# Letting the halves of a weight stream take turns at several byte places of their buffers

## The chip, the core and the metric

The kernel runs on one core of a Trainium2 chip. The metric is the device time of one execution in microseconds (us). The kernel before takes 1099.93 us, the median of 3 runs (1099.71 to 1100.56). The engines are named as in the profile: PE is the matrix engine (TensorE), PEld its weight load, DVE the vector engine, ACT the scalar engine, POOL the general-purpose engine (GpSimd), SP the engine whose queue issues most transfers.

## The reference: what is computed

Two layers of a decoder trunk over 256 tokens of width 1024, all in f32. Each layer does

```
x = x + W_out( sum_i sigmoid(G_i(h)) * P_i(mixer_i(h)) )     h = rmsnorm(x), four mixers, one wide projection w_in
x = x + cross_attention(rmsnorm(x), rmsnorm(mem))            4 heads, 256 memory tokens
x = x + (relu(rmsnorm(x) @ w_up)**2) @ w_down                hidden width 4096
```

and a last rmsnorm ends the trunk. Nearly all of the arithmetic is products of a 1024-wide (or 4096-wide) weight with the 256 tokens. The mixers (latent attention, a gated MLP over chunks, gated linear attention, a delta-rule network) add many small products and elementwise steps.

## The kernel before, in words

**The weight stream.** All large weights lie in one array in the order in which they are used, 168 halves of 128 x 1024 f32 in each layer, two halves to a transfer of 1 MB. The function `half()` hands out the next one. It takes a buffer `wh` and a buffer `wl` (four of each in rotation). ACT copies the raw half into `wh` in the format fp32r that PE multiplies (L191), DVE writes what is left over, raw minus `wh`, into `wl` (L194). A product in nearly full f32 precision is then three matmuls, `mm3` at L197 to L200: `wh` with the operand's high part, `wh` with its low part, `wl` with its high part. PE loads the 128 x 128 weights anew for each matmul.

**The products.** `gemm` takes the weights as the stationary side and streams 256 tokens of the operand past them: 8 chunks of 128 columns in a half, three matmuls each, so 24 matmuls of 128x256 to a half. `gemm_tok` turns the sides round: 128 tokens are stationary and 512 columns of the weights stream past, 12 matmuls of 128x512 to a half. The operands (`hh`, `hl`, `ah`, `al`, `mh`, `ml`, `brh`, `oh` and so on) are tiles of 2048 bytes in each partition.

**The places.** A `wh` or `wl` buffer has 1024 floats and 512 bytes of slack in each partition, 4608 bytes. The half lies in it at an offset of 0 to 480 bytes, the place. `PLACE` has one place for each stage and layer, `weights(stage)` sets it when the stage begins, and `half()` uses it for `wh` and `wl` alike. The buffers are nine times 512 bytes apart, a chunk of weights is 512 bytes long, the two halves of an operand tile are 1024 bytes and the tiles of one pool 2048 bytes apart. So within a stage the distance in bytes from the weights of a matmul to the operand that streams past them is the same for all, up to multiples of 512, and the place alone sets it.

**The stages**, with their halves in each layer and their places before, in bytes (layer 0, layer 1). All but tok, v and the second layer's down are `gemm`:

| stage | halves | what | place before | matmuls |
|---|---|---|---|---|
| z | 18 | input projections of the mixers | 384, 256 | 432 of 128x256 |
| tok | 6 | token-major projections, two small factors of the attention | 448, 448 | 48 of 128x512, some of 128x256 |
| gate | 32 | branch gates, interleaved with the mixers' small work | 256, 384 | 768 of 128x256 |
| k | 8 | keys of the memory | 128, 384 | 192 of 128x256 |
| br | 8 | branch projections | 384, 256 | 192 of 128x256 |
| out, q, o | 8 each | output, queries, attention output | 288, 352, 416 and 224, 480, 288 | 192 of 128x256 each |
| v | 8 | values of the memory | 448, 0 | 96 of 128x512 |
| up | 32 | MLP, first matrix | 384, 256 | 768 of 128x256 |
| down | 32 | MLP, second matrix | 256, 448 | layer 0: 768 of 128x256; layer 1: 384 of 128x512 |

**What sets the order.** A scheduler orders the instructions of each engine at build time. The splits of L191 and L194 have raised priority, so that they run ahead of their use. Transfers of the stream are issued from SP's queue. The mixers run as generators beside the gate stage: only there are the large products interleaved with many small ones.

Of the kernel before, what the change touches and what calls it, by code (L numbers as in the profile page):

```python
# [42 lines left out]
PAD = 48  # L43


SLACK = 512
PLACE = [
    dict(z=384, tok=448, gate=256, k=128, br=384, out=288, q=352, v=448, o=416, up=384, down=256),
    dict(z=256, tok=448, gate=384, k=384, br=256, out=224, q=480, v=0, o=288, up=256, down=448),
]  # L50
N_PIECE = 44

# [12 lines left out]
def decoder(ctx: ExitStack, tc: tile.TileContext, ws, xn_d, xt_d, mem_d, pos_d, fin_d, par_d, cst_d, msk_d, out_d):  # L65
# [12 lines left out]
    def nm(s):  # L78
        uid[0] += 1
        return f"{s}_{uid[0]}"  # L80
# [59 lines left out]
    for j in range(4):  # L140
        c = slice(1024 * (j % 2), 1024 * (j % 2) + 1024)
# [27 lines left out]
    class Stream:  # L169
        i = 0  # L170
        raw = None
        place = PLACE[0]["z"]

    def half(parts=1):
        if Stream.i % 2 == 0:
            if Stream.i < 4:
                Stream.raw = raw0[Stream.i // 2]
            else:
                Stream.raw = wp.tile([P, 2048], F32, tag="wr", name=nm("wr"), bufs=3)
                nc.sync.dma_start(Stream.raw, ws[Stream.i // 2])  # L180
        o = 1024 * (Stream.i % 2)
        Stream.i += 1
        r = Stream.raw[:, o : o + 1024]
        wh, wl = (wp.tile([P, 1024 + SLACK // 4], F32R, tag=n, name=nm(n), bufs=4) for n in ("wh", "wl"))
        b = Stream.place // 4
        wh, wl = wh[:, b : b + 1024], wl[:, b : b + 1024]
        n = 1024 // parts
        for c in range(0, 1024, n):
            p = slice(c, c + n)
            with tc.high_priority(offset=WP):  # L190
                i = S.activation(wh[:, p], r[:, p], AF.Copy)  # L191
                if Stream.i <= 4:
                    tc.keep_in_program_order(i)
                V.tensor_tensor(wl[:, p], r[:, p], wh[:, p].bitcast(F32), op=ALU.subtract)  # L194
        return wh, wl
# [6 lines left out]
    def lead4(xh, xl, evac, pieces):  # L202

        bk = [pg.tile([P, 2, T], F32, tag="g", name=nm("g")) for _ in range(2)] + [bank() for _ in range(2)]
        for j in range(4):
            w = half(2 if j == 0 else 1)
            pieces(j)
            for m in range(4):
                for i in range(2):
                    k = 2 * j + i  # L210
                    c = slice(256 * m + 128 * i, 256 * m + 128 * i + 128)
                    mm3(bk[m][:, 0], w[0][:, c], w[1][:, c], xh(k), xl(k), k == 0, k == 7)
        for p in range(2):
            evac(p, [(slice(m, m + 1), bk[2 * p + m][:, 0:1]) for m in range(2)])

    def gemm(xh, xl, nk, npair, evac, lead=False, tail=False, first=0):

        for p in range(first, npair):  # L220
            apart = (lead and p == 0) or (tail and p == npair - 1)
            if apart:
                bk = [pg.tile([P, 2, T], F32, tag="g", name=nm("g")) for _ in range(2)]
                parts = [(slice(m, m + 1), bk[m][:, 0:1]) for m in range(2)]
                out = [bk[m][:, 0] for m in range(2)]
            else:
                ps = pg.tile([P, 2, T], F32, tag="g", name=nm("g"))
                parts = [(slice(0, 2), ps)]
                out = [ps[:, m] for m in range(2)]
            if lead and p == 0:  # L230
                w = [half() for _ in range(2)]
                order = [(m, k) for kp in range(0, 8, 2) for m in range(2) for k in (kp, kp + 1)]
            else:
                w = [None, None]
                order = [(m, k) for m in range(2) for k in range(nk)]
            for m, k in order:
                if k % 8 == 0 and not (lead and p == 0):
                    w[m] = half()
                c = slice(128 * (k % 8), 128 * (k % 8) + 128)
                mm3(out[m], w[m][0][:, c], w[m][1][:, c], xh(k), xl(k), k == 0, k == nk - 1)  # L240
            evac(p, parts)
# [196 lines left out]
    def layer(l):  # L438
# [18 lines left out]
        def weights(stage):  # L457
            Stream.place = PLACE[l][stage]

# [1010 lines left out]
```

## Time and profile before

| what | value |
|---|---|
| median of 3 runs | 1099.93 us |
| the profiled execution's own time | 1101.14 us |
| its span from first to last instruction | 1098.5 us |
| granted clock of PE over the span | 0.996 |
| busy: PE, PEld, DVE, ACT, POOL | 98%, 94%, 74%, 53%, 18% |
| read from HBM | 182.75 MB, 167 GB/s over the span |

The profile is one execution. A row of the view of groups names line, engine, operation, output<-inputs and shape, then the count, the busy time in us with the mean of one in ns, and the idle time of the engine just before. Matmuls are pipelined: each has a duration of some 280 ns, and yet the next one starts after some 115 ns, so the rate is read from how many start in a stretch of time, not from durations. The view of stretches gives for each stretch (us from the span's start) its length, PE's busy time and the number of its instructions that overlap the stretch, the granted clock, the share of the DMA engines and what they moved.

### The profile page before, as it was taken

How to read it: one execution, taken by the hardware profiler on the slowest of the kernel's cores; microseconds unless marked ns; L12 is line 12 of the kernel's file. 1: busy time of each engine (PE TensorE's matmuls, PEld its weight loads, DVE VectorE, ACT ScalarE, POOL GpSimd, SP SyncE). 2: the span in 40 equal slices, each digit the busy share in tenths (PEclk: the TensorE clock that was granted, in tenths of full speed). 3: DMA queues.
4: the chain of work that ended last, by engine and by line, in shares of the span. 5: the costliest groups of instructions: out<-in, count | busy, mean ns of one | idle time of the engine just before them, and what ended most of it. 6: DMA issues, size and time to landing. Idle time of an engine off the chain costs nothing.

```text
span 1098.5 us, 20696 instructions
## 1 busy us (share of the span) xinstructions
PE 1074.4 (98%) x8494; PEld 1032.4 (94%) x8494; DVE 812.5 (74%) x1419; ACT 584.2 (53%) x875; POOL 194.6 (18%) x170
## 2 busy tenths in 40 slices
PE   8989999999999999999999999999999999999996
PEld 8979998899998999999999899999999899999885
DVE  6999857779866876655679997686797768665454
ACT  6565554554645655544454746554455555555342
POOL 6234005108200200000101420320351001010000
PEclk9999999999999999999999999999999999999999
DMA  9442523354544455555545444244445345554551
GB/s 354 163 179 111 204 104 121 110 193 156 191 153 154 154 192 192 192 192 193 192 183 192 155 154 154 103 150 151 174 177 204 122 152 193 186 194 177 192 192 38
DMA packets 28319, 185.13 MB, mean 169 GB/s; under 512 B 3392, under 2 KB 3648, under 8 KB 6976
## 3 DMA queue, kind: packets, MB, share of 16 engines
q1 hardware_dynamic: 26208, 179.09, 44.9%
q10 hardware_dynamic: 2016, 4.72, 1.3%
q8 instruction: 66, 1.08, 0.4%
q14 instruction: 29, 0.24, 0.1%
HBM read 182.75 MB, written 1.05 MB: 167 GB/s over the span
## 4 chain that ended last, share of the span: by engine, by line
PE 86%; DVE 8%; ACT 2%; DMA 2%; issue 1%; POOL 0%; DVEq 0%; ACTq 0%
PE g L198 25%; PE g L199 25%; PE g L200 25%; DVE wl L194 2%; DMA mr<-memt 1%; PE ps L198 1%; PE ps L199 1%; PE ps L200 1%; ACT wh L191 1%; PE ps L666 1%; PE ps L662 1%; DVE cv L539 1%; DVE qt L861 0%; DMA wr<-ws 0%; PE ps L972 0%
## 5 line engine op out<-in xcount | busy, mean ns | idle before, releaser
L194 DVE TENSOR_TENSOR wl<-wr,wh 128x1024 fp32r<-128x1024 f32 (+1 forms) x337 | 416.9, 1239 | 187.8 <-ACT wh L191 186.6
L191 ACT ACTIVATE wh<-wr 128x1024 fp32r<-128x1024 f32 (+1 forms) x337 | 355.1, 1057 | 344.3 <-PE g L199 238.8
L200 PE MATMUL g<-hh,wl 128*128 128x256 f32 x1152 | 325.1, 282 | 3.5 <-DVE wl L194 3.5
L198 PE MATMUL g<-hh,wh 128*128 128x256 f32 x1152 | 323.8, 282 | 1.9 <-ACT gt L1097 1.4
L199 PE MATMUL g<-hl,wh 128*128 128x256 f32 x1152 | 322.9, 280 | 0.0
L200 PEld LDWEIGHTS g<-hh,wl 128*128 128x128 f32 x1152 | 216.5, 188 | 5.5 <-DVE wl L194 4.5
L198 PEld LDWEIGHTS g<-hh,wh 128*128 128x128 f32 x1152 | 216.5, 188 | 3.1 <-ACT gt L1097 1.8
L199 PEld LDWEIGHTS g<-hl,wh 128*128 128x128 f32 x1152 | 217.3, 189 | 0.4 <-issue 0.2
L338 POOL TENSOR_TENSOR sq<-sq,sq 128x512 f32<-128x512 f32 x14 | 21.2, 1513 | 350.5 <-ACT sq L330 350.3
L198 PE MATMUL g<-xh,wh 128*128 128x256 f32 x272 | 75.5, 281 | 2.0 <-ACT xh L311 2.0
L199 PE MATMUL g<-xl,wh 128*128 128x256 f32 x272 | 75.8, 281 | 0.0
L200 PE MATMUL g<-xh,wl 128*128 128x256 f32 x272 | 74.9, 280 | 0.0
L198 PE MATMUL g<-ah,wh 128*128 128x256 f32 x256 | 70.7, 276 | 0.0
L199 PE MATMUL g<-al,wh 128*128 128x256 f32 x256 | 70.7, 276 | 0.0
L200 PE MATMUL g<-ah,wl 128*128 128x256 f32 x256 | 70.7, 276 | 0.0
L198 PEld LDWEIGHTS g<-xh,wh 128*128 128x128 f32 x272 | 51.3, 190 | 2.4 <-ACT xh L311 2.4
L1113 POOL TENSOR_TENSOR gt<-gt,gt 128x512 f32<-128x512 f32 x16 | 35.6, 2228 | 91.0 <-DVE gt L1112 90.0
L199 PEld LDWEIGHTS g<-xl,wh 128*128 128x128 f32 x272 | 51.2, 189 | 0.1
L200 PEld LDWEIGHTS g<-xh,wl 128*128 128x128 f32 x272 | 51.0, 189 | 0.0
L200 PE MATMUL g<-wh,al 128*128 128x512 f32 x128 | 49.5, 389 | 0.0
L199 PE MATMUL g<-wl,ah 128*128 128x512 f32 x128 | 49.5, 389 | 0.0
L198 PE MATMUL g<-wh,ah 128*128 128x512 f32 x128 | 49.4, 390 | 0.0
(500 smaller groups left out, 2332.6 us busy)
## 6 DMA issues: line engine op xcount, KB each, us to landing
wr<-ws SPq DMA_DIRECT2D x166, 1024.0 KB, 4.8
wr<-ws ACTq DMA_DIRECT2D x4, 512.0 KB, 7.6
mr<-memt ACTq DMA_DIRECT2D x8, 256.0 KB, 4.5
par<-par SPq DMA_DIRECT2D x2, 778.0 KB, 7.0
x<-xt SPq DMA_DIRECT2D x3, 256.0 KB, 7.7
cst<-cst SPq DMA_DIRECT2D x1, 588.0 KB, 8.7
gf<-fin SPq DMA_DIRECT2D x2, 256.0 KB, 5.3
yt<-yg ACTq DMA_DIRECT2D x2, 256.0 KB, 2.5
```

What stands on the lines that cost most here:

```text
L191: i = S.activation(wh[:, p], r[:, p], AF.Copy)
L194: V.tensor_tensor(wl[:, p], r[:, p], wh[:, p].bitcast(F32), op=ALU.subtract)
L198: PE.matmul(out, ah, bh, start=start, stop=False)
L199: PE.matmul(out, ah, bl, start=False, stop=False)
L200: PE.matmul(out, al, bh, start=False, stop=stop)
L338: G.tensor_tensor(acc, acc, sq, op=ALU.add)
L539: V.scalar_tensor_tensor(cv[:, c, d], zc[p][:, c, 0 : T - 3 + k], col(o + k), cv[:, c, d], op0=ALU.mult, op1=ALU.add)
L662: PE.matmul(xp[:, h], M[:, h], Tm[:, h], start=True, stop=True)
L666: PE.matmul(up[:, h], X[t][:, h], U[:, h], start=True, stop=True)
L1113: G.tensor_tensor(gt[m][0], gt[m][0], gt[m][1], op=ALU.add)
```

## The change

The place becomes a list of pairs for each stage. Each half takes the next entry of its stage's list, by its number in the stream: the first number of a pair is the place of `wh`, the second that of `wl`. A list of one entry is a fixed place; a list of two or four makes the halves take turns. The sizes of the buffers stay as they are.

```diff
 SLACK = 512
+ONE, TOK = [(256, 256)], [(448, 448)]
 PLACE = [
-    dict(z=384, tok=448, gate=256, k=128, br=384, out=288, q=352, v=448, o=416, up=384, down=256),
-    dict(z=256, tok=448, gate=384, k=384, br=256, out=224, q=480, v=0, o=288, up=256, down=448),
+    dict(z=[(0, 0), (256, 256)], tok=TOK, gate=[(256, 256), (384, 384)], k=[(0, 0), (128, 128)], br=[(128, 128), (384, 384)],
+         out=ONE, q=ONE, v=TOK, o=ONE, up=[(256, 384)], down=[(0, 0), (128, 128), (256, 256), (384, 384)]),
+    dict(z=[(256, 256), (384, 384)], tok=TOK, gate=[(0, 256)], k=[(384, 384), (0, 0)], br=[(0, 0), (256, 256)],
+         out=ONE, q=ONE, v=TOK, o=ONE, up=[(0, 0), (256, 256)], down=TOK),
 ]
...
-        b = Stream.place // 4
-        wh, wl = wh[:, b : b + 1024], wl[:, b : b + 1024]
+        b, c = (n // 4 for n in Stream.place[Stream.i % len(Stream.place)])
+        wh, wl = wh[:, b : b + 1024], wl[:, c : c + 1024]
```

In the built program every engine has the same instructions in the same order as before, with the same shapes. Only the addresses differ from which matmuls read their weights (or, in `gemm_tok`, their streamed side) and to which L191 and L194 write.

By stage: two places 256 bytes apart take turns in z of layer 0, in br of both layers and in up of layer 1. Two places 128 bytes apart (384 and 0 are 128 apart, up to a multiple of 512) take turns in gate and k of layer 0 and in z and k of layer 1; down of layer 0 goes round four places in steps of 128. In gate of layer 1 and up of layer 0 the place is fixed, and `wh` and `wl` lie at different ones, 256 and 128 bytes apart. The stages out, q and o are at a fixed 256 in both layers, tok, v and the second layer's down at 448; of these v of layer 1 (0 before) is moved, tok and down are not.

## The prediction

> **What bounds the kernel now.** I read the page's busy times first, then its chain of waits by line, then the groups, and last the stretches, which decided.
>
> ```profile
> PE 1074.4 (98%) x8494; PEld 1032.4 (94%) x8494; DVE 812.5 (74%) x1419; ACT 584.2 (53%) x875; POOL 194.6 (18%) x170
> PE g L198 25%; PE g L199 25%; PE g L200 25%; DVE wl L194 2%; DMA mr<-memt 1%; PE ps L198 1%; PE ps L199 1%; PE ps L200 1%; ACT wh L191 1%; PE ps L666 1%; PE ps L662 1%; DVE cv L539 1%; DVE qt L861 0%; DMA wr<-ws 0%; PE ps L972 0%
> L200 PE MATMUL g<-hh,wl 128*128 128x256 f32 x1152 | 325.1, 282 | 3.5 <-DVE wl L194 3.5
> L198 PE MATMUL g<-hh,wh 128*128 128x256 f32 x1152 | 323.8, 282 | 1.9 <-ACT gt L1097 1.4
> L200 PE MATMUL g<-ah,wl 128*128 128x256 f32 x256 | 70.7, 276 | 0.0
> ```
>
> Three quarters of the span are the three matmuls of `mm3` one behind the other, with next to no idle time before them. So the time is the number of these matmuls times their spacing, and the change can only act on the spacing. The last two rows hint that it isn't one number: the matmuls on `ah` have a mean of 276 ns, those on `hh` 282, in the same shape.
>
> The stretches give it exactly. Each row is a piece of a stage with little in it but the large matmuls: its length, PE busy (so many instructions), clock, DMA share, GB/s. A matmul lasts some 280 ns, so about two that began earlier are counted at the left edge; I take the length over the count less two.
>
> ```profile
> 20.00:35.00 15.00, 15.00 (x130) 1.00 0.82 308
> 42.00:56.00 14.00, 14.00 (x126) 1.00 0.51 185
> 223.00:243.00 20.00, 20.00 (x173) 1.00 0.62 213
> 255.00:265.00 10.00, 10.00 (x87) 1.00 0.59 209
> 278.00:291.00 13.00, 13.00 (x112) 1.00 0.49 173
> 298.00:315.00 17.00, 17.00 (x144) 1.00 0.53 186
> 363.00:373.00 10.00, 10.00 (x88) 1.00 0.68 224
> 380.00:460.00 80.00, 80.00 (x681) 1.00 0.52 188
> 466.00:551.00 85.00, 85.00 (x753) 1.00 0.53 188
> 567.00:582.00 15.00, 15.00 (x135) 1.00 0.39 141
> 584.00:601.00 17.00, 17.00 (x148) 1.00 0.62 219
> 649.00:656.00 7.00, 7.00 (x64) 1.00 0.16 46
> 663.00:672.00 9.00, 9.00 (x80) 1.00 0.47 171
> 755.00:780.00 25.00, 25.00 (x215) 1.00 0.49 176
> 813.00:826.00 13.00, 13.00 (x112) 1.00 0.47 167
> 832.00:850.00 18.00, 18.00 (x154) 1.00 0.53 194
> 896.00:908.00 12.00, 12.00 (x104) 1.00 0.53 180
> 916.00:1000.00 84.00, 84.00 (x715) 1.00 0.53 192
> ```
>
> The two long ones: up of layer 0 (380 to 460) runs at 80/679 = 117.8 ns, down of layer 0 (466 to 551) at 85/751 = 113.2 ns. Clock, DMA share and GB/s are alike, so neither throttle nor transfers part them. At places that are multiples of 128 (all but out, q, o) every row is near one of these two values: z of layer 0 first 117.2 then 112.9, z of layer 1 112.8 then 116.4, gate of layer 1 112.9 then 115.4, k 117.0 and 117.4, br of layer 0 117.6, up of layer 1 117.8. I call them the **fast** and the **slow rhythm**, 4.6 ns apart. At the odd places out, q and o have rates of their own: layer 0 118.2, 119.7, 116.3; layer 1 118.2, 118.4, 117.6 ns.
>
> Two things matter for a change of places. First, one fixed place carries both rhythms (z and gate of layer 1), so the place doesn't fix the rhythm; where the stream was thrown decides. Second, a change of place throws it, even without a pause. At 465.5 us up hands over to down, place 384 to 256, and no idle time stands in the groups of the stretch 455 to 475:
>
> ```profile
> L200 PE MATMUL g<-hh,wl 128*128 128x256 f32 x31 | 8.6, 279 | 0.0
> L198 PE MATMUL g<-hh,wh 128*128 128x256 f32 x30 | 8.4, 280 | 0.0
> L198 PE MATMUL g<-ah,wh 128*128 128x256 f32 x28 | 7.7, 276 | 0.0
> ```
>
> The mean falls from 279 or 280 (slow) to 276 (fast) with the first matmuls of down, and stays there for the whole stage. A pause throws it too. In up of layer 1 the stream is fast until small matmuls of a statistic come between, and slow behind them:
>
> ```profile
> 909.79 0.28 PE L200 MATMUL g<-oh,wl 128*128 128x256 f32 x1
> 909.91 0.28 PE L198 MATMUL g<-hh,wh 128*128 128x256 f32 x1
> 910.02 0.28 PE L199 MATMUL g<-hl,wh 128*128 128x256 f32 x1
> 910.13 0.28 PE L200 MATMUL g<-hh,wl 128*128 128x256 f32 x1
> ...
> 914.33 0.50 PE L352 MATMUL ps<-cst,sq 128*128 128x1 f32 x4
> ...
> 915.48 0.28 PE L198 MATMUL g<-hh,wh 128*128 128x256 f32 x1
> 915.60 0.28 PE L199 MATMUL g<-hl,wh 128*128 128x256 f32 x1
> 915.72 0.28 PE L200 MATMUL g<-hh,wl 128*128 128x256 f32 x1
> ```
>
> These are starts in us. From the handover on (o at 288 to up at 256, between 909.79 and 909.91) the steps are 0.11, after the statistic at 914.33 they are 0.12. No change of place follows in that stage, and it stays slow to its end (916 to 1000).
>
> **The change part by part.** No instruction comes, goes or moves on any engine or queue, and no wait is added. The new addresses of L191 and L194 lie under PE's work: in the row of busy times DVE has 26% and ACT 47% of the span free, and all waits on L194 in the largest group are 3.5 us. I cost them at nothing; if every split became slower by 10 ns and none of it were hidden, 336 splits would be 3.4 us. What is left is the spacing, stage by stage. A half has 24 matmuls, so moving one stage of 768 from slow to fast is worth 768 x 4.6 ns = 3.5 us, one of 192 is worth 0.9.
>
> *Turns that differ by 128 bytes* throw the stream once in each half, every 2.8 us. Down of layer 0 shows that the fast rhythm, once reached, holds for 768 matmuls at a fixed place. The open question is whether it also survives a throw. Nothing before shows a throw out of the fast rhythm by a 128-byte step; the one throw by 128 from slow with a clear end went to fast (465.5 us), while gate to k in layer 0 (256 to 128) ends in the slow k of row 223 to 243. If throws from slow sometimes reach fast, and fast survives them, the turns work as a ratchet. Bounds: k of both layers are slow throughout (rows 223 and 755), 2 x 0.9 = 1.8 us; z of layer 1 and gate of layer 0 are partly fast, I take half slow, (432 + 768)/2 x 4.6 = 2.8 us; up of layer 0, where `wl` lies 128 from `wh` so that each triple is thrown, 3.5 us. All of it is 8.1 us, none of it is 0, and a loss is not excluded: the fast half of z and gate (2.8 us) and all of down (3.5 us) could fall to slow. I take three quarters of the gain, 6.1 us, and no loss in down, because the only clear throw ended fast and the turns give many tries.
>
> *Turns that differ by 256 bytes* (z and gate of one layer each, br twice, up of layer 1). From k to br in layer 0 the place goes 128 to 384, and the slow rhythm goes on as if nothing had been changed (117.6 ns in row 255 to 265). So I expect a step of 256 to throw nothing, and these stages to keep what their first matmuls bring: 0, with bounds of a loss of 3.5 us (z of layer 0, fast from 42 us on, and gate of layer 1 are half fast at most) and a gain of the 3.5 us of up of layer 1 plus 3.5 for gate of layer 1.
>
> *out, q and o at a fixed 256.* Over the fast 113.2 they now spend 5.0 + 6.5 + 3.1 + 5.0 + 5.2 + 4.4 = 29.2 ns a matmul, times 192 = 5.6 us if all become fast. If all become slow, each gets 4.6 less of it: 1.6 ns x 192 = 0.3 us. At a fixed 256 the trace has both, fast at once from 909.91 us and slow from 915.48 us on. I take the middle, 3.0 us.
>
> *v of layer 1 from 0 to 448.* The groups of three stretches, v of layer 1 (852 to 880, place 0), v of layer 0 (322 to 342, place 448) and down of layer 1 (1002 to 1086, place 448):
>
> ```profile
> L199 PE MATMUL g<-wl,mh 128*128 128x512 f32 x32 | 12.8, 399 | 0.0
> L199 PE MATMUL g<-wl,mh 128*128 128x512 f32 x28 | 11.0, 393 | 0.0
> L199 PE MATMUL g<-wl,ah 128*128 128x512 f32 x123 | 47.5, 389 | 0.0
> ```
>
> Means of 399, 393 and 389 ns: some 5 ns a matmul would go, 96 of them, 0.5 us.
>
> The sum: 6.1 + 3.0 + 0.5 = 9.6 us off. The profiled execution took 1101.14 us, 2.6 outside its span, and would come to 1091.5; it lies 1.2 above the median of the runs, so for the median I say **1090.3 us**.
>
> **A rule that speaks against it.** The Trainium skill, "SBUF — State Buffer", section "Who interferes with whom", gives PE two read ports, one for the streamed operand and one for the weight load, and calls them independent; it also says that PE never waits on anyone. By that rule no place could matter and the time would stay at 1099.9. The trace disagrees: q and o of layer 0 do the same work at 119.7 and 116.3 ns. It may still be right that places of one kind don't differ, which is the second rival below.
>
> **The rivals.**
>
> *The throws empty the fast rhythm.* Each turn by 128 throws a fast stream back to slow as easily as the reverse, and slow is where it comes to rest: the statistic at 914.3 us did just that, and the long slow stretches (380 to 460, 916 to 1000) show that slow is stable too. Then down of layer 0 loses 3.5, the fast halves of z and gate (z and gate of both layers at most a half: 2400/2 x 4.6) up to 5.5, and out, q, o and v still give 0.8: +8.2 at the worst, +5 if half of z and gate was slow anyway in the new order of pauses, so 1105. It decides when a throw from fast ends slow more often than a throw from slow ends fast. Against it: the handovers at 465.5 and 909.9 us both ended fast.
>
> *Places of one kind don't differ.* All multiples of 128 act alike, a turn throws nothing, and the handover at 465.5 us was due to something else there (other operand tiles, a waited semaphore). Then only out, q, o and v change: 0.3 to 5.6 and 0.5, so 3.5 us off, 1096.4; if out, q and o come up slow it is 0.8, too little to tell. For it: both rhythms occur at 256 and at 384, and 128 to 384 passed unseen.
>
> *Everything goes fast.* Turns of both kinds ratchet, in all stages: 8.1 + 5.6 + 0.5 + br and z of layer 0 (384 x 4.6 + 216 x 4.6 = 2.8) + up of layer 1 and half or more of gate (3.5 + 2.5) = 23 off, 1077. Against it: the pauses among the mixers' small matmuls keep throwing the gate stage.
>
> *No place matters*, by the mechanism that PE's two reads don't disturb each other: 1099.9.
>
> **How the numbers follow.** Forecast 0.45; everything fast 0.12; places alike 0.20, of which a quarter too small to tell; emptied 0.15; no place matters 0.08. A measurement of this kernel tells some 0.2%, 2.2 us, from no change. Faster: 0.45 + 0.12 + 0.15 = 0.72; same: 0.05 + 0.08 = 0.13; slower: 0.15. The range goes from 1080 (two thirds of the way to everything fast) to 1102 (the first part of the emptied case), which leaves out about 0.2. The forecast's own range is 1085 to 1095.
>
> **What would show it.** In the profile after, up of layer 0 should come to down's 113 ns with a mean of 276 in most of its halves, k of both layers likewise, and down of layer 0 should keep its 276. If down shows 279 or more, the emptied case holds. If k and up of layer 0 stay at 279 or 280 while out, q and o change, the places are alike. The count and order of instructions, DVE's and ACT's busy time and the idle time on L194 should stay; if L191 or L194 become slower, I overlooked the splits. The forecast is wrong if up of layer 0 has a spacing above 118, since then placing `wl` apart from `wh` has a price that no row here shows.

## The result and the profile after

The changed kernel takes **1091.16 us** (median of 3 runs, 1090.66 to 1092.46), 0.9921 of the time before, with a 95% interval of 0.9899 to 0.9944. The forecast was 1090.3 us. The profiled execution took 1090.66 us, with a span of 1088.3 us at a granted clock of 0.997; the span is 10.2 us shorter than before. The medians differ by 8.8 us: the profiled execution before lay 1.2 us above its median, the one after 0.5 us below.

The page's row of busy times, and from its costliest groups the two splits, a matmul on `hh` and one on `ah` (the change moves every line number below it by 4, so L194 is now L198 and L200 is L204):

```profile
PE 1064.5 (98%) x8494; PEld 1020.9 (94%) x8494; DVE 812.7 (75%) x1419; ACT 583.8 (54%) x875; POOL 197.6 (18%) x170
L198 DVE TENSOR_TENSOR wl<-wr,wh 128x1024 fp32r<-128x1024 f32 (+1 forms) x337 | 415.3, 1235 | 182.9 <-ACT wh L195 181.2
L195 ACT ACTIVATE wh<-wr 128x1024 fp32r<-128x1024 f32 (+1 forms) x337 | 355.1, 1057 | 332.9 <-PE g L203 233.8
L204 PE MATMUL g<-hh,wl 128*128 128x256 f32 x1152 | 324.0, 282 | 3.4 <-DVE wl L198 3.4
L204 PE MATMUL g<-ah,wl 128*128 128x256 f32 x256 | 70.7, 276 | 0.0
```

The counts are the same, DVE and ACT are busy as long as before, the idle time on `wl` is 3.4 us (3.5 before). PE's busy time fell by 9.9 us: what changed is its spacing.

The same view of stretches as in the prediction, PE alone, at the places of the same stages (length over the count less two):

```profile
20.00:35.00 15.00, 14.72 (x130) 1.00 0.78 308
42.00:56.00 14.00, 14.00 (x121) 1.00 0.42 156
222.00:242.00 20.00, 20.00 (x178) 1.00 0.58 211
292.00:311.00 19.00, 19.00 (x165) 1.00 0.52 174
350.00:369.00 19.00, 19.00 (x169) 1.00 0.36 117
378.00:456.00 78.00, 78.00 (x691) 1.00 0.52 190
460.00:543.00 83.00, 83.00 (x734) 1.00 0.53 191
548.00:562.00 14.00, 14.00 (x126) 1.00 0.67 249
575.00:597.00 22.00, 22.00 (x191) 1.00 0.53 194
752.00:772.00 20.00, 20.00 (x175) 1.00 0.46 166
798.00:817.00 19.00, 19.00 (x168) 1.00 0.48 176
822.00:840.00 18.00, 18.00 (x156) 1.00 0.53 183
912.00:990.00 78.00, 78.00 (x665) 1.00 0.54 193
```

Up of layer 0 (378 to 456) is at 113.2 ns, 117.8 before; down of layer 0 (460 to 543) stays at 113.4; up of layer 1 (912 to 990) stays at 117.6. k of layer 0 (222) came to 113.6, k of layer 1 (752) to 115.6, o of layer 0 (350) to 113.8, while q of both layers (292 and 822) is at 116.6 and 116.9.

Why one up is fast and the other slow stands in the order of time. Both are interrupted by the four small matmuls of the same statistic. The view of starts, PE alone, for up of layer 0 (`wl` lies 128 bytes from `wh`) and for up of layer 1 (turns of 256):

```profile
374.92 0.50 PE L356 MATMUL ps<-cst,sq 128*128 128x1 f32 x4
375.60 0.28 PE L203 MATMUL g<-hl,wh 128*128 128x256 f32 x1
375.84 0.28 PE L203 MATMUL g<-hl,wh 128*128 128x256 f32 x1
...
376.86 0.28 PE L203 MATMUL g<-hl,wh 128*128 128x256 f32 x1
...
904.09 0.50 PE L356 MATMUL ps<-cst,sq 128*128 128x1 f32 x4
904.77 0.28 PE L203 MATMUL g<-hl,wh 128*128 128x256 f32 x1
905.01 0.28 PE L203 MATMUL g<-hl,wh 128*128 128x256 f32 x1
...
906.07 0.28 PE L203 MATMUL g<-hl,wh 128*128 128x256 f32 x1
```

From 375.60 to 375.84 there are two steps of 0.12 us, as slow as from 904.77 to 905.01. From there nine matmuls take 1.02 us in layer 0, 113.3 ns each, and 1.06 us in layer 1, 117.8 ns each. The pause throws both streams; the one with the 128 bytes between its two weight operands is fast again two matmuls later, the other stays slow for the rest of its stage.

All stages together, worked out from the starts in the trace: the sum, over the steps of a stage from each large matmul to the next matmul on PE, large or small, of what lies above 113.33 ns (226.67 ns for 512 columns). I call it the excess. Steps more than 16 ns above that are pauses, and what they have above it stands in the row "pauses"; the small matmuls' own time is in neither. The last two rows are the lengths of gate and br in both layers together, from a stage's first large matmul to that of the next stage. Us; the columns behind "after" are experiments told below.

| stages | before | after | fixed 256 | turns of 256 | turns of 128 | wl 128 from wh | wl 256 from wh | down at 384 |
|---|---|---|---|---|---|---|---|---|
| z, layers 0, 1 | 1.04, 1.08 | 0.83, 0.70 | 0.71, 1.41 | 0.60, 1.41 | 0.85, 0.70 | 0.22, 0.14 | 1.24, 1.41 | 1.90, 1.08 |
| gate, layers 0, 1 | 2.06, 2.95 | 1.94, 1.96 | 2.29, 1.93 | 1.98, 1.88 | 1.72, 1.70 | 0.90, 0.77 | 2.09, 2.68 | 2.26, 2.45 |
| k, both | 1.70 | 0.74 | 0.77 | 0.80 | 0.36 | 0.16 | 0.80 | 1.71 |
| br, both | 1.59 | 0.44 | 0.30 | 0.32 | 0.55 | 0.34 | 0.95 | 1.61 |
| out, q, o, both | 5.50 | 1.64 | 1.50 | 2.26 | 0.34 | 0.22 | 1.52 | 5.32 |
| up, layer 0 | 3.41 | 0.03 | 3.24 | 3.24 | 0.22 | 0.03 | 3.24 | 3.41 |
| down, layer 0 | 0.00 | 0.00 | 3.42 | 3.42 | 0.00 | 0.00 | 3.42 | 3.41 |
| up, layer 1 | 3.24 | 3.24 | 3.24 | 3.24 | 0.03 | 0.02 | 3.24 | 3.24 |
| tok with the small factors, v, down of layer 1 | 1.22 | 0.88 | 0.83 | 0.81 | 0.91 | 0.91 | 0.83 | 1.24 |
| sum | 23.8 | 12.4 | 19.6 | 19.9 | 7.4 | 3.7 | 21.4 | 27.6 |
| pauses | 25.5 | 26.5 | 27.2 | 27.3 | 28.5 | 29.2 | 25.6 | 23.9 |
| span | 1098.5 | 1088.3 | 1096.2 | 1096.7 | 1084.5 | 1081.4 | 1096.5 | 1100.6 |
| length of gate | 289.1 | 288.9 | 289.3 | 289.1 | 288.4 | 287.8 | 289.4 | 289.0 |
| length of br | 46.6 | 46.5 | 46.5 | 46.5 | 46.6 | 46.5 | 46.6 | 46.6 |

From before to after the spacing gave 11.4 us and the pauses took 1.0 back, 10.4 us together; the span fell by 10.2. The pauses grew by 1.0 us in br and 0.8 us in gate; z of layer 0 and tok had 1.1 us less, which is chance: a kernel below with the same z (up of layer 0 put back) has 1.2 us more pauses there than the changed kernel. So br gained 1.15 us in spacing and became 0.1 us shorter, and gate gained 1.1 us and became 0.2 us shorter. The last two rows show the same in every column: the lengths of these two stages hardly follow their spacing.

### The profile page after: what moved, and what is told of

Its sections match the earlier page's. It is cut to its first block, busy times and chain, and to the rows that moved or that the text cites. A ratio compares the mean times of both kernels' runs of the same rounds, so it can differ in the third digit from the quotient of the medians.

```text
span 1088.3 us, 20696 instructions
## 1 busy us (share of the span) xinstructions
PE 1064.5 (98%) x8494; PEld 1020.9 (94%) x8494; DVE 812.7 (75%) x1419; ACT 583.8 (54%) x875; POOL 197.6 (18%) x170
## 3 DMA queue, kind: packets, MB, share of 16 engines
q8 instruction: 66, 1.08, 0.4%
## 4 chain that ended last, share of the span: by engine, by line
PE 81%; DVE 11%; ACT 3%; DMA 2%; issue 1%; POOL 1%; ACTq 0%; DVEq 0%; POOLq 0%
PE g L202 24%; PE g L204 24%; PE g L203 24%; DVE wl L198 3%; DMA mr<-memt 2%; DVE qt L865 1%; PE ps L202 1%; ACT wh L195 1%; PE ps L203 1%; PE ps L204 1%; DVE gt L1116 1%; PE ps L666 1%; PE ps L670 1%; DMA wr<-ws 1%; DVE mgl L1124 1%
## 5 line engine op out<-in xcount | busy, mean ns | idle before, releaser
L198 DVE TENSOR_TENSOR wl<-wr,wh 128x1024 fp32r<-128x1024 f32 (+1 forms) x337 | 415.3, 1235 | 182.9 <-ACT wh L195 181.2
L195 ACT ACTIVATE wh<-wr 128x1024 fp32r<-128x1024 f32 (+1 forms) x337 | 355.1, 1057 | 332.9 <-PE g L203 233.8
L204 PE MATMUL g<-hh,wl 128*128 128x256 f32 x1152 | 324.0, 282 | 3.4 <-DVE wl L198 3.4
L204 PEld LDWEIGHTS g<-hh,wl 128*128 128x128 f32 x1152 | 216.4, 188 | 5.6 <-DVE wl L198 4.4
L204 PE MATMUL g<-xh,wl 128*128 128x256 f32 x272 | 74.5, 279 | 0.0
L204 PE MATMUL g<-ah,wl 128*128 128x256 f32 x256 | 70.7, 276 | 0.0
L204 PEld LDWEIGHTS g<-xh,wl 128*128 128x128 f32 x272 | 50.8, 189 | 0.0
L204 PE MATMUL g<-wh,al 128*128 128x512 f32 x128 | 49.5, 389 | 0.0
```

The source lines that it names most:

```text
L204: PE.matmul(out, al, bh, start=False, stop=stop)
```

## The experiments

The theory was that of the prediction, sharpened by the trace after: between places that are multiples of 128 a stream has two stable rhythms; a step of 128 bytes in the distance from weights to operand throws it, mostly to fast and not back; a step of 256 bytes does nothing; pauses throw it to either side. The rivals were that 256 throws as well, that the fixed places of out, q and o did the work, that any turning does it, and that the place in memory counts rather than the distance.

### Which step throws the stream: five kernels with one rule for all stages

Each puts all stages that go through `gemm` on one list, `GEMM`, and keeps tok, v and down of layer 1 at 448. The first, against the changed kernel (whose own lists in `PLACE` go; they are left out here):

```diff
-ONE, TOK = [(256, 256)], [(448, 448)]
+GEMM, TOK = [(256, 256)], [(448, 448)]
 PLACE = [
...
+    dict(z=GEMM, tok=TOK, gate=GEMM, k=GEMM, br=GEMM, out=GEMM, q=GEMM, v=TOK, o=GEMM, up=GEMM, down=GEMM),
+    dict(z=GEMM, tok=TOK, gate=GEMM, k=GEMM, br=GEMM, out=GEMM, q=GEMM, v=TOK, o=GEMM, up=GEMM, down=TOK),
 ]
```

> Every stage that streams the 256 tokens past the weights has the one fixed place 256 for wh and wl; tok, v and the second down stay at 448. No turns. Theory (only steps of 128 bytes throw the stream, and the slow rhythm once entered stays until a throw or a pause): up of layer 0 and of layer 1 are slow from the statistic among their first matmuls on (117.8 ns), down of layer 0 takes over the slow rhythm since nothing throws it (117.8 ns, 3.4 us lost against before), out, q and o are near after's: some 1097, 1094 to 1100. Rival (places of one kind are alike, the gain came from leaving the odd places): as after, 1091.

Measured: 1098.08 us, ratio 0.9987 (0.9977 to 0.9996). The stretches 294 to 312 (q of layer 0), 380 to 455 (up of layer 0), 470 to 540 (down of layer 0) and 925 to 985 (up of layer 1), PE alone:

```profile
294.00:312.00 18.00, 18.00 (x155) 1.00 0.56 184
380.00:455.00 75.00, 75.00 (x639) 1.00 0.52 184
470.00:540.00 70.00, 70.00 (x597) 1.00 0.52 182
925.00:985.00 60.00, 60.00 (x512) 1.00 0.54 191
```

117.6, 117.7, 117.6 and 117.6 ns: slow, down of layer 0 too, which was fast before. It lost 3.4 us; out, q and o gave 4.0, k, br and gate 3.0 together. New places alone bring the sum from 23.8 to 19.6 us, the change brings it to 12.4, so most of its gain has another cause. In k, br and gate, though, the new places alone give as much as the change does or nearly so.

The second lets the halves take turns 256 bytes apart, the third puts `wl` 256 bytes from `wh`:

```diff
-GEMM, TOK = [(256, 256)], [(448, 448)]
+GEMM, TOK = [(0, 0), (256, 256)], [(448, 448)]
```

> The same stages take turns at 0 and 256, wh and wl alike. Theory (a step of 256 throws nothing): as the fixed place, 1094 to 1100, no half-to-half alternation of the rhythm, up of both layers slow behind the statistic. Rival (any alternation throws the stream): as turns of 128, 1087 or so, with up and down of layer 0 fast.

```diff
-GEMM, TOK = [(256, 256)], [(448, 448)]
+GEMM, TOK = [(0, 256)], [(448, 448)]
```

> As the kernel with wl 128 bytes beside wh in every token-streaming stage, but wh at 0 and wl at 256, so 256 bytes apart. Theory (only a step of 128 disturbs the slow rhythm): like the fixed place, 1098, with up of both layers slow behind the statistic and down of layer 0 slow. Rival (any difference between wh and wl breaks it): 1084, everything fast.

Measured: 1098.90 us, ratio 0.9994 (0.9985 to 1.0004), and 1098.87 us, ratio 0.9985 (0.9976 to 0.9995). The same stretches of up and down of layer 0 and up of layer 1, of the kernel with the turns and of the kernel with `wl` apart:

```profile
380.00:455.00 75.00, 75.00 (x639) 1.00 0.52 183
470.00:540.00 70.00, 70.00 (x597) 1.00 0.53 183
925.00:985.00 60.00, 60.00 (x512) 1.00 0.53 193
```

```profile
380.00:455.00 75.00, 75.00 (x639) 1.00 0.52 184
470.00:540.00 70.00, 70.00 (x597) 1.00 0.52 183
925.00:985.00 60.00, 60.00 (x512) 1.00 0.53 191
```

The counts equal those of the fixed place. Turning as such does nothing, and neither do 256 bytes between the two weight operands. The next two are the same with 128 bytes:

```diff
-GEMM, TOK = [(256, 256)], [(448, 448)]
+GEMM, TOK = [(256, 256), (384, 384)], [(448, 448)]
```

> The same stages take turns at 256 and 384, wh and wl alike. Theory (a step of 128 moves a slow stream to fast in about every second handover and never a fast one to slow): up and down of layer 0 and up of layer 1 fast within a few halves, q in both layers too, gate still partly slow because of its pauses: 1087, 1084 to 1090. Rival (throws act both ways): down of layer 0 falls to slow in part, 1092 or more. Rival (places alike): as the fixed place.

```diff
-GEMM, TOK = [(256, 256)], [(448, 448)]
+GEMM, TOK = [(256, 384)], [(448, 448)]
```

> Every one of these stages has wh at 256 and wl at 384, fixed, as up of layer 0 has in the changed kernel. Theory (in each triple the weights step by 128 bytes and back, so that the slow rhythm cannot close on itself): every stage at 113.3 ns, behind each pause too within two or three matmuls; of the 12.4 us that the changed kernel still loses to slower spacing some 10 go: 1081, 1079 to 1084. Rival (up of layer 0 was fast in the changed kernel by the luck of its pauses): up of layer 1 or q stay slow behind the statistic as they do now, 1088 to 1096.

Measured: 1086.38 us, ratio 0.9876 (0.9860 to 0.9893), with the turns, and 1083.93 us, ratio 0.9858 (0.9844 to 0.9873), with `wl` apart. The four stretches of the one and of the other:

```profile
294.00:312.00 18.00, 18.00 (x161) 1.00 0.53 187
380.00:455.00 75.00, 75.00 (x663) 1.00 0.56 197
470.00:540.00 70.00, 70.00 (x620) 1.00 0.54 191
925.00:985.00 60.00, 60.00 (x532) 1.00 0.57 202
```

```profile
294.00:312.00 18.00, 18.00 (x160) 1.00 0.60 223
380.00:455.00 75.00, 75.00 (x664) 1.00 0.55 196
470.00:540.00 70.00, 70.00 (x620) 1.00 0.56 196
925.00:985.00 60.00, 60.00 (x533) 1.00 0.58 202
```

All of them are at 113.0 to 113.9 ns. Up of layer 1 gains 3.2 us that the change itself had left, and q is fast. The starts also tell how the stream behaves where one half hands over to the next. Counted are handovers within a stage with no other instruction and no pause from five steps ahead of it to thirteen behind. A side counts as fast when all its steps are at most 115 ns and as slow when all are at least 116.5, by the five steps ahead and by the last nine behind. Left out are the halves at the start of a stage that are worked on in turn:

```
kernel, step of the place                   from fast: stays fast    from slow: becomes fast
fixed 256, none                              54 of  54                 1 of 134
turns of 256                                 51 of  51                 0 of 136
turns of 128, 384 to 256                     74 of  74                19 of  25
turns of 128, 256 to 384                     76 of  76                 0 of  10
changed kernel, 128 or 384 to 0 or 256       21 of  21                10 of  15
changed kernel, 0 or 256 to 128 or 384       26 of  26                 0 of   5
```

This is the ratchet of the prediction, counted, and it has a direction. A step from 128 or 384 back to 0 or 256 lifts a slow stream at two to three of four handovers, the opposite step at none of 15, and neither has thrown a fast one. It isn't that every second half is a better one: k of layer 1 in the changed kernel has its pairs the other way round, and its lifts (384 to 0, two of three) stand at the other handovers. The trace before agrees: 384 to 256 at 465.5 us lifted the stream, and 256 to 128 from gate to k of layer 0, which the prediction left unexplained, did not.

With `wl` 128 from `wh` the step comes twice in each triple, once in each direction, and no slow stretch is longer than eight steps: z and gate fall from 0.70 to 1.72 us a stage with the turns to 0.14 to 0.90.

The theory expected 1081 here, some 10 us off the changed kernel's excess. The spacing gave 8.7 (20.1 of the 23.8 before), but against before the pauses grew by 3.7 us: 2.7 in gate (16.4 us in both layers before, 19.1 here) and 1.1 in br. Gate saves 3.3 us in spacing and is only 1.4 us shorter (0.4 in the second profile of this kernel, told below), br saves 1.25 and is 0.1 us shorter. So something other than PE's spacing holds the length of these two stages. That it is the mixers beside gate, and in br the elementwise work on the products (`gt`, the one wait of PE that the view of waits names there), is argued; no run varied that work.

### One stage at a time

Before, with down of layer 0 left at the place of up, so that the handover between them has no step:

```diff
-    dict(z=384, tok=448, gate=256, k=128, br=384, out=288, q=352, v=448, o=416, up=384, down=256),
+    dict(z=384, tok=448, gate=256, k=128, br=384, out=288, q=352, v=448, o=416, up=384, down=384),
```

> The kernel before, with one place changed: down of layer 0 at 384 instead of 256, so that the handover from up (384) no longer steps by 128. Theory (the step threw the stream into the fast rhythm at the handover): down of layer 0 stays at 117.8 ns, 768 x 4.45 ns = 3.4 us more, 1103. Rival (something else at that handover, such as the other operand tiles or the waited semaphores, made it fast): 1100 and down at 113.3 ns.

Measured: 1103.06 us, ratio 1.0026 (1.0016 to 1.0035). Down of layer 0 in the stretch 470 to 540:

```profile
470.00:540.00 70.00, 70.00 (x597) 1.00 0.52 186
```

117.6 ns where before had 113.3. This settles the handover at 465.5 us, on which the prediction rests: the same operand tiles and the same waits without the step, here 384 to 256, stay slow. The run also shows how much is chance: z of layer 0, whose instructions and places are those of before, had an excess of 1.90 us against 1.04, since pauses threw it otherwise.

The changed kernel, with up of layer 0 put back:

```diff
-         out=ONE, q=ONE, v=TOK, o=ONE, up=[(256, 384)], down=[(0, 0), (128, 128), (256, 256), (384, 384)]),
+         out=ONE, q=ONE, v=TOK, o=ONE, up=[(384, 384)], down=[(0, 0), (128, 128), (256, 256), (384, 384)]),
```

> The changed kernel with one part undone: up of layer 0 at 384 for wh and wl alike, as before the change, all else kept. Theory (wl 128 bytes beside wh is what kept up of layer 0 fast): up is slow from the statistic on, some 700 matmuls x 4.45 ns = 3.2 us more than the changed kernel, 1094.3; down of layer 0, which takes turns by 128, is still fast but for its first half or two. Rival (up was fast because it came fast from o): 1091, up at 113.3 ns.

Measured: 1095.88 us, ratio 0.9959 (0.9944 to 0.9974), 4.7 us above the changed kernel. Up and down of layer 0:

```profile
380.00:455.00 75.00, 75.00 (x640) 1.00 0.51 183
470.00:540.00 70.00, 70.00 (x620) 1.00 0.54 191
```

Up is slow (117.6 ns, excess 3.41 us, 3.38 more than in the changed kernel), down is fast. So this one stage is worth 3.4 us. Another 1.2 us stand in two stages that are the same in both kernels and come ahead of it: o of layer 0 has 0.79 against 0.03 us, br of layer 0 has 0.79 against 0.36. Down takes up the slow rhythm from up and has an excess of 0.11 us before its first handover, 128 to 256, lifts it.

### Place or distance

A fixed place that is 64 bytes off, alone and with the filler `PAD` (in f32 words) ahead of the operands raised from 48 to 64, which moves the operands 64 bytes on too and so restores the distance:

```diff
-GEMM, TOK = [(256, 256)], [(448, 448)]
+GEMM, TOK = [(320, 320)], [(448, 448)]
```

> The fixed place 256 replaced by a fixed 320 in all these stages, 64 bytes on. Theory (what counts is the distance from the weights to the streamed operand, modulo 128; the two small factors of the attention, at 448, that is 64 off the multiples of 128, run at 120 ns): one rhythm of 120 ns in all the stages, 6600 matmuls times 2 to 7 ns more than the fixed 256, some 1120. Rival (only steps between successive weights matter): 1098, as at the fixed 256.

```diff
-PAD = 48
+PAD = 64
...
-GEMM, TOK = [(256, 256)], [(448, 448)]
+GEMM, TOK = [(320, 320)], [(448, 448)]
```

> The fixed place 320 again, and the pool of the operand tiles moved 64 bytes on as well (a spacer in front of it is 64 floats long instead of 48), so that the distances are those of the fixed 256. Theory (distance): 1098 again, with 113.3 and 117.8 ns and no 120. Rival (the absolute place of the weights counts): as the fixed 320 without the moved pool, some 1120.

Measured, one run each: 1112.05 us and 1095.94 us. Up and down of layer 0 and up of layer 1 at place 320:

```profile
380.00:455.00 75.00, 75.00 (x634) 1.00 0.52 183
470.00:540.00 70.00, 70.00 (x592) 1.00 0.51 181
925.00:985.00 60.00, 60.00 (x501) 1.00 0.52 188
```

And with the operands moved as well, with down of layer 1 (1000 to 1080) as a fourth row:

```profile
380.00:455.00 75.00, 75.00 (x661) 1.00 0.53 188
470.00:540.00 70.00, 70.00 (x620) 1.00 0.55 195
925.00:985.00 60.00, 60.00 (x512) 1.00 0.55 198
1000.00:1080.00 80.00, 80.00 (x345) 1.00 0.41 146
```

Alone, 64 bytes give 118.7, 118.6 and 120.2 ns, slower than the slow rhythm, and no fast stretch anywhere. The expectation of 1120 took one rhythm of 120 for all of it, which was too much: some stretches run at 118.7 and others at 120. With the operands moved too, 113.8, 113.3 and 117.6 ns are back: both rhythms, at the place that had neither. The stages left at 448 now have lost their old distance, and pay: down of layer 1 is at 80/343 = 233.2 ns a matmul of 512 columns, in the changed kernel at 226.7. The attention's two small factors, left at 448 too but turned as in `gemm`, gain: their steps fall from 119.8 and 119.6 ns in the changed kernel to 114.9 and 113.9. So the distance between weights and operand counts, not the place; each of the two kernels was timed once, and what was read is far above the noise.

### A better version

The kernel with `wl` 128 bytes from `wh` was timed again, beside one that gives the attention's two small factors the same pair as the gate:

```diff
+        weights("gate")
         run = [dn(), others()]
```

> The kernel with wl 128 bytes beside wh in all token-streaming stages once more, beside the one before it on the same chip: 1083.9, and every stage as in its first profile.

> The kernel with wl 128 bytes beside wh in all token-streaming stages, and the two small factors of the attention (84 matmuls of 128x256 in the two layers, at 448 until now and at 120 ns) given the same pair of places, 256 and 384. Theory: 84 x 6 ns = 0.5 us less than without it, 1083.4, in the profile 113.3 ns for these matmuls. Rival: they sit in the part where the small mixers set the pace, and nothing is gained, 1083.9.

Measured: 1084.76 us, ratio 0.9863 (0.9847 to 0.9879), and 1084.03 us, ratio 0.9856 (0.9841 to 0.9870). The factors' excess fell by 0.4 us (tok 0.37 and 0.28 to 0.15 and 0.09), but the intervals overlap: no gain that these runs can tell. The simpler one is the best version found, 1.4% below before, and by the medians 6.4 to 7.2 us below the change.

## Why the prediction was right

The time came within 1 us, for the reason given, though not by all of its terms. That it came so close is partly luck: terms that were too large and gains that no term held cancel.

- **Nothing but the spacing.** Right: the splits have 1235 and 1057 ns, the idle time on `wl` 3.4 us.
- **Turns of 128, 6.1 us.** Right in mechanism, too large: 4.8 (up of layer 0 3.4, k 1.0, z of layer 1 0.4, gate of layer 0 0.1). The mis-sized term is the one for z of layer 1 and gate of layer 0: the prediction gave them up to 2.8 us, and they gave 0.5. In gate the mixers' pauses throw the stream faster than one handover in 2.8 us can lift it; only a step in each triple does, as the kernel with `wl` 128 from `wh` shows (0.90 us instead of 1.94). The prediction also took every handover for a try; only the step back to 0 or 256 is one. And k's 1.0 us is not the turns' alone: the fixed 256 has 0.9 there without any, though the trace after does show slow become fast at k's handovers.
- **No loss in down.** Right: 0.00 us through 31 handovers.
- **Turns of 256, 0 us.** As a statement on the turns it is right: in the five-kernel comparison they do the same as a fixed place. The stages that carry them still gained 2.35 us (gate of layer 1 1.0, br 1.15, z of layer 0 0.2). The fixed 256 has most of that without a turn (gate of layer 1 1.93, br 0.30), so it comes from the places that stages begin and end at and from pauses. Which of the two wasn't separated. Little of it reached the time: br became 0.1 us shorter, gate of layer 1 too.
- **out, q and o, 3.0 us.** 3.9, within its bounds: out and o came up fast, q slow in both layers, behind the same kind of statistic as up of layer 1.
- **v of layer 1, 0.5 us.** 0.4.
- What no term held: the pauses took 1.0 us back. The terms that fell short and those that were left out cancel: 4.8 + 2.35 + 3.9 + 0.4 - 1.0 = 10.4 by the profiled executions, against 9.6; by the medians it is 8.8.

The rivals. That throws empty the fast rhythm falls with 150 of 150 fast handovers. That places of one kind are alike falls with the pairs of kernels at 128 and 256 bytes, 12.5 us apart with the turns and 14.9 with `wl` apart. That no place matters falls with 1098.08 against 1112.05 us for places 256 and 320. The Trainium skill, "SBUF — State Buffer", section "Who interferes with whom", says that PE never waits on anyone; between the engines no run here tests it, and read as covering PE's own two operands it fails to foretell this case, since the distance between them moved the spacing from 113.3 to 120 ns. Everything fast was nearly reached, by another kernel, and there the pauses kept it from 1077 (the excess left is 3.7 us, the pauses 3.7 us more than before).

**What stays open** is why a stream has two rhythms at one distance and why a step of 128 lifts it in one direction only. The runs tell which distances and which steps, not what in PE or in the memory is met twice.

## What to carry to other kernels

Where PE is busy all the time, read the starts of its matmuls, not their durations or its busy share: here 4% of the rate stood between two stretches of the same shape, clock and transfer load. The distance in bytes from the stationary to the streamed operand is worth a trial of its own, with the operands' addresses kept in known steps. If the stream has a slow rhythm that it falls into after pauses, let two operands that follow each other closely lie at distances that differ by 128 bytes: a step in each triple keeps the fast rhythm, a step in each half does so only where pauses are rare. Ask first whether a stage's length follows its spacing at all: in gate and br, where PE was busy 95% of the time and more, it hardly did.

## What the runs showed of the hardware that was not expected

- The step of 128 works in one direction. In the kernel with turns of 128, 384 to 256 lifted 19 of 25 slow streams and 256 to 384 none of 10, and neither threw one of 150 fast ones.
- 256 bytes are nothing at all: 187 handovers with that step, and not one changed the rhythm.
- 64 bytes off has rhythms of its own, 118.7 and 120 ns, and none at 113.3.
- Matmuls with 512 columns depend on the distance too. With the stationary operand moved by 64 bytes, down of layer 1 went from 226.7 to 233.2 ns; with the streamed weights moved from 0 to 448, v of layer 1 went from 231.9 to 227.9.
- The lowest spacing of 256 columns in any run is 113.3 ns. The Trainium skill, "TensorE: Matmul & The Clock Gate", section "Back-to-back issue gap", gives N/2.4 + 2.5 ns for an isolated warm matmul, 109.2 as an estimate for 256 columns, and says that in a stream of weight loads and matmuls both set the spacing; the 4.1 ns above the estimate would fit the second, but no run here separates the two.
